# Sliding-window attention: one turned block of summed probabilities, and values as block and difference

## The chip, the core and the metric

The kernel runs on one core of a Trainium2 chip. The metric is the device time of one launch in microseconds (us); lower is better. Engines are called as the profile calls them: PE (TensorE), DVE (VectorE), ACT (ScalarE), POOL (GpSimd), SP (the queue that issues most DMAs). A time written as "at 245 us" counts from the start of the profiled span.

## What is computed

One inference step of one layer of a hybrid decoder for a prompt of 1024 tokens and 8 sequences of 4 sample tokens. The input is normalised and modulated by a condition, multiplied by one wide matrix (`w_in`), and goes through two branches: an mLSTM (matrix memory, 4 heads, chunks of 128 tokens) and an attention over a sliding window (8 query heads in groups of 4 over 2 key heads, head size 64, window 128, with a learned sink per head). Both are gated, multiplied by their output matrices and merged, and a last matrix and norm give `y`. The change touches the prompt's attention alone:

```python
dist = q_pos[:, :, None] - k_pos[:, None, :]
mask = (dist >= 0) & (dist < WINDOW) & (k_pos[:, None, :] >= 0)
s = jnp.where(mask[None, :, None, None], s, -jnp.inf)
mx = jnp.maximum(jnp.max(s, axis=-1, keepdims=True), sink)
p = jnp.exp(s - mx)
den = jnp.sum(p, axis=-1, keepdims=True) + jnp.exp(sink - mx)
o = jnp.einsum('bnkgqs,bnskd->bnqkgd', p / den, v.astype(f32))
```

A block of 128 queries sees two blocks of keys, the preceding one ("far") and its own ("near"). With window 128, query i sees the far keys j > i and the near keys j <= i. So in each row the two masks are complementary: where one block has a probability, the other has zero.

## The kernel before

The program is one long instruction stream, written by Python code. The large products run one after another on PE: the keys and values (`ak`, `av`), four query jobs (`aq` 0 to 3), eight jobs for the memory heads (`mq`, `mk`, `mv`), and from about 282 us pairs of jobs done as seven block products each (`block_products`, `Pair`), then the output matrices. Each job is 8 x 3 products for each of three pieces of columns (`piece`).

Everything smaller is fed in between by a planner, the class `Side`. It holds generators in streams: "m" (the chain of gate factors, then the four memory heads), "a" (`kv_turn`, then 16 attention units), "x" (`sum_blocks` and later loads), "s" (sample attention, then four sample heads), "g" (`ada_gate`). A stream has a maximum of generators alive and a least gap between two starts. A generator yields a lag and the PSUM banks that its next visit needs; the planner keeps its own clock, `side.now`, which products advance by estimated durations (`mm`, `tr`), and at each `tick` steps those generators whose lag has passed and whose banks are free by its own reckoning. So the order of PE's instructions is fixed when the program is written. `side.until(condition)` advances the planner's clock without large products until the condition holds; `hook` calls it ahead of the block products that read `sum_blocks`' operands ("t2", "t1"), ahead of the query gates (all 16 units done), and ahead of the head gates (enough sample heads done: five for the last).

PSUM has four pairs of banks, tagged `g`, `a`, `b` and `o`. Tiles of SBUF with tag `half` come from 43 buffers. `store` puts a DMA off by 4.0 of the planner's clock; `dma` issues at once, after any put-off store to the same tensor.

A `unit(g, b0)` does two query blocks of query group g, for both key heads (kv 0 and 1):

1. loads of the queries (`q`, in `qv`), three key blocks (`kT`) and the value blocks (`vn`, one in `kv_`, two in `qv`); lag 12.0
2. four score products into banks `a`; DVE adds the mask and takes maxima; then `nmx`
3. ACT: exponentials with sums (`den`)
4. DVE: `den` and its reciprocal; probabilities times 1/den, kv 0 on DVE, kv 1 on ACT, 256 columns each; lag 7.0
5. eight transposes (six where b0 = 0, which has no far block for its first query block), four for each kv into a bank `b`; ACT and DVE copy them back
6. eight products with values (six where b0 = 0) into a bank `o`; ACT copies, and the result is stored.

`kv_turn` transposes the values once for all units and keeps them in DRAM (`vnD`).

A memory `head(h)` goes through its chunks in three groups (loads, `prep`, `stage_a` to `stage_c3`), each a chain of small operations on ACT and DVE with products in between; the sample heads start when the last of the four is done.

Of the kernel before, what the change touches and what calls it, by code (L numbers as in the profile page):

```python
# [10 lines left out]
F32 = mybir.dt.float32  # L11
# [100 lines left out]
class Side:  # L112
# [4 lines left out]
    def __init__(self, each, limits, quiet):  # L117
        self.each, self.free = each, {}
        self.now, self.last, self.quiet, self.products = 0.0, 0.0, quiet, 0
        self.streams = {n: {"max": m, "gap": g, "wait": [], "live": [], "next": 0.0} for n, (m, g) in limits.items()}  # L120

    def add(self, stream, gen, banks=""):
# [15 lines left out]

    def tick(self):
        self.each()  # L140
        for st in self.streams.values():
            if st["wait"] and len(st["live"]) < st["max"] and self.now >= st["next"]:
                self.begin(st)
        used, visit = set(), self.now >= self.last + self.quiet
        for item in sorted((i for st in self.streams.values() for i in st["live"]), key=lambda i: i[1]):
            banks = set(item[2])
            if self.now < item[1] or used & banks or (banks and not visit) or any(self.now < self.free.get(b, 0) for b in banks):
                continue
            used |= banks
            for b in banks:  # L150
                self.free[b] = self.now + (6.0 if "+" in banks else HOLD[b])
            n = self.products
            self.step(item)
            if self.products > n:
                self.last = self.now
# [17 lines left out]
def body(tc, a):  # L173
    nc = tc.nc
    with ExitStack() as ctx:
# [11 lines left out]
        def pb(shape, name):  # L187
            return ps.tile(shape, F32, tag="b", bufs=2, name=name)
# [52 lines left out]
        def dma(out, in_, late=False):  # L241
            stores(in_.tensor)
            issue(out, in_, late)

        def issue(out, in_, late=False):
            ins = nc.sync.dma_start(out, in_)
            ins = getattr(ins, "ins", ins)
# [5 lines left out]
        side = Side(stores, {"m": (2, 35.0), "a": (5,8.0), "x": (2, 0.0), "s": (1, 0.0), "g": (1, 0.0)}, 1.5)  # L253
        def mm(out, lhsT, rhs, start, stop, share=1, more=False):
            n = int(np.prod(rhs.shape[1:]))
            side.now += max(n, 250) / 2400 if rhs.dtype == F32R else max(n * 4 // share, 128) / 2400
            side.products += 1
            in_order(nc.tensor.matmul(out, lhsT, rhs, start=start, stop=stop, skip_group_check=more))  # L258

        def tr(out, in_, idn):  # L260
            side.now += 0.11
            side.products += 1
            in_order(nc.tensor.transpose(out, in_, idn))
# [460 lines left out]
        def by_block(t):  # L724
            return t.rearrange("p (c q e) -> p c q e", q=4, e=32)
# [14 lines left out]
        kD, vnD = dp.tile([128, SEQ], F32, name="kD"), dp.tile([128, 8, 128], F32, name="vnD")  # L740
        qD = [dp.tile([128, SEQ], F32, name=f"qD{g}") for g in range(4)]

        def rope_load(p):
# [30 lines left out]
        def kv_turn():  # L774
            kl, kTs, vT, kns, vns = at.pop("kl"), at["kTs"], at.pop("vT"), ht([128, 128], "kns")[:NS], at["vns"]
            for p, n in enumerate((3, 3, 2)):
                tp = pb([128, 3, 128], f"vtp{p}")
                for j in range(n):
                    tr(tp[:, j], vT[p][:, j * 128:(j + 1) * 128], ident)
                vn = ht([128, 3, 128], f"avn{p}")  # L780
                S.copy(vn[:, :n], tp[:, :n])
                dma(vnD[:, 3 * p:3 * p + n], vn[:, :n])
                if p < 2:
                    yield 4.0, "b"
            dma(a["v_p"], vn[:, 1])
# [12 lines left out]
            dma(a["v_s"][124:128].rearrange("t b e -> b t e"), vns)  # L798
# [8 lines left out]
        def unit(g, b0):  # L807
# [2 lines left out]
            n0 = 1 if b0 == 0 else 0  # L810
            qv, kv_ = ht([128, 4, 128], "uqv"), ht([128, 4, 128], "ukv")
            q, kT = qv[:, 0:2].rearrange("p c e -> p (c e)"), kv_[:, 0:3].rearrange("p c e -> p (c e)")
            vn = kv_[:, 3], qv[:, 2], qv[:, 3]
            dma(q, qD[g][:, b0 * 128:b0 * 128 + 256])
            dma(kT[:, n0 * 128:], kD[:, (b0 - 1 + n0) * 128:(b0 + 2) * 128])
            dma(qv[:, 2:4], vnD[:, b0:b0 + 2])
            if b0:
                dma(vn[0], vnD[:, b0 - 1])
            yield 12.0, sc_bank[1]
            p = [ht([128, 2, 256], f"p{kv}") for kv in range(2)]  # L820
            mx = sm([128, 4], "mx", 3)
# [16 lines left out]
            for kv in range(2):  # L838
                for i, lo in enumerate(los):
                    j = 2 * kv + i  # L840
                    S.activation(p[kv][:, i, lo:], p[kv][:, i, lo:], AF.Exp, bias=nmx[:, j:j + 1],
                                 accum_out=den[:, j:j + 1])
            yield 3.0, ""
            V.tensor_tensor(den, den, nmx[:, 4:8], op=ALU.add)
            V.reciprocal(den, den)
            for kv in range(2):
                for i, lo in enumerate(los):
                    j = 2 * kv + i
                    if kv:
                        S.activation(p[kv][:, i, lo:], p[kv][:, i, lo:], AF.Copy, scale=den[:, j:j + 1])  # L850
                    else:
                        V.tensor_scalar(p[kv][:, i, lo:], p[kv][:, i, lo:], den[:, j:j + 1], None, op0=ALU.mult)
            yield 7.0, "b"
            pT = [t.rearrange("p i (j e) -> p (i j) e", e=128) for t in p]
            for kv in range(2):
                pt = pb([128, 4, 128], f"pt{g}_{b0}_{kv}")
                for j in range(n0, 4):
                    tr(pt[:, j], p[kv][:, j // 2, j % 2 * 128:j % 2 * 128 + 128], ident)
                if kv:
                    V.tensor_copy(pT[kv][:, n0:], pt[:, n0:])  # L860
                else:
                    S.copy(pT[kv][:, n0:], pt[:, n0:])
            yield 5.0, "o"
            oT = po([128, 2, 128], f"oT{g}_{b0}")
            for j in range(n0, 4):
                i, hf = divmod(j, 2)
                for kv in range(2):
                    r = slice(64 * kv, 64 * kv + 64)
                    mm(oT[r, i], vn[i + hf][:, r], pT[kv][:, j], start=(hf == 0 or b0 + i == 0), stop=(hf == 1))
            c0 = b0 * 128  # L870
            o = qv[:, 0:2].rearrange("p c e -> p (c e)")
            S.copy(o, oT.rearrange("p c e -> p (c e)"))
            store(oD[g][:, c0:c0 + 256], o)
            units_done.append((g, b0))
# [146 lines left out]
        def across(h, n, src, c0):  # L1021
            m = src.shape[1]
            t = ht([128, 512], f"{n}t")[:, :m]
            V.transpose(t, src)
            for b in range(0, 128, 32):
                nc.gpsimd.dma_start(mN[n][h][c0:c0 + m, b:b + 32].rearrange("(t p) e -> p t e", p=32), t[b:b + 32].rearrange("p (t e) -> p t e", e=32))  # L1026

        def head(h):
            an, wend, dec, fl = st["an"], st["wend"], st["dec"], st["fl"]
# [88 lines left out]
            def stage_c3(p):  # L1118
                m = len(GROUPS[p])
                ns, (d, r) = w_[p]  # L1120
                for i in range(m):
                    V.tensor_scalar(ns[:, i, 0:128], ns[:, i, 0:128], d[:, i:i + 1], r[:, i:i + 1], op0=ALU.mult, op1=ALU.mult)
                y = ht([128, 384], "yt")[:, :m * 128]
                V.transpose(y.rearrange("p (c e) -> p c e", e=128), ns[:, :m, 0:128])
                c0 = GROUPS[p][0]
                for b in range(4):
                    nc.gpsimd.dma_start(yhD[h][c0:c0 + m].rearrange("c (q i) (b e) -> b i c q e", i=32, e=32)[b], by_block(y[32 * b:32 * b + 32]))  # L1127
# [607 lines left out]
        def hook(n, i):  # L1735
# [404 lines left out]
```

## Time and profile before

| | |
|---|---|
| time, median of 3 runs | 861.15 us (860.39 to 861.27) |
| time of the profiled execution | 857.75 us |
| its span, first to last instruction | 855.9 us |
| mean granted PE clock | 0.992 |
| instructions | 15332 |
| transposes in the units (`pt`) | 120, from 111.2 to 260.4 us |
| value products in the units (`oT`) | 240 instructions, from 118.0 to 274.1 us |

The profile's page gives for each engine its busy time and its share of the span; then the span in 40 slices, a digit being the busy share of a slice in tenths (9 for 90% or more). A line of a group reads: source line, engine, operation, output<-inputs, shapes, count | busy us, mean ns | idle time of the engine ahead of it, and what ended it. A line of one tile gives durations as min/median/max ns, and the first and last start. A line of the timeline gives start, duration, engine and operation, and in brackets the idle time before it with its releaser. Waits are listed as engine and tile <- what released it: total us, number, longest. Nearly all operations are recorded in a helper, so they share the line of it (L219, L246, L258, L263) and are told apart by their tiles.

### The profile page before, as it was taken

The numbers are of one execution on the slowest core, as the hardware profiler recorded it, in microseconds if no ns is written. First come the engines' busy times: TensorE is split into PE (matmuls) and PEld (weight loads), VectorE is DVE, ScalarE is ACT, GpSimd is POOL, SyncE is SP. The second block draws the span as 40 slices with busy tenths as digits, with TensorE's granted clock in tenths as the row PEclk, the third lists the DMA queues.
The fourth block names the chain that finished last, engine by engine and source line by source line (L and its number), as shares of the span: only waits on it lengthen the run. The fifth ranks groups of instructions, "written<-read, shape, count | busy, mean of one in ns | idle before, by whom it ended". The sixth has DMA issues, their size and how long they took to land. (4 is left out here: it accounts for less than half of the span.)

```text
span 855.9 us, 15332 instructions
## 1 busy us (share of the span) xinstructions
PE 822.3 (96%) x5139; PEld 686.6 (80%) x5139; DVE 604.1 (71%) x1596; ACT 390.5 (46%) x963; POOL 174.7 (20%) x236
## 2 busy tenths in 40 slices
PE   6899999999999989999999999999999999999984
PEld 3689988789789778888887777777788999967863
DVE  3787785555687778668666565978766669857987
ACT  4672356545564543555444454434443333233334
POOL 0220000330341434211111000000012032532563
PEclk9999999999999999999999999999999999999998
DMA  9995549459756765664444335553436974273322
GB/s 326 366 356 183 150 137 291 134 125 294 214 153 203 214 170 151 194 198 135 129 115 130 115 111 162 160 150 89 116 99 203 345 254 137 82 247 99 111 99 104
DMA packets 125347, 150.82 MB, mean 176 GB/s; under 512 B 29057, under 2 KB 81409, under 8 KB 125237
## 3 DMA queue, kind: packets, MB, share of 16 engines
q1 hardware_dynamic: 121044, 143.55, 53.5%
q0 software_dynamic: 4224, 6.30, 3.6%
q8 instruction: 40, 0.66, 0.3%
q14 instruction: 39, 0.31, 0.1%
HBM read 109.73 MB, written 41.08 MB: 176 GB/s over the span
## 5 line engine op out<-in xcount | busy, mean ns | idle before, releaser
L1127 POOL DMA_DIRECT2D yhD<-yt x48 | 28.9, 608 | 108.3 <-DVE yt L219 86.3
L258 PE MATMUL g_w_ao<-ya,wh_w_ao 128*128 128x384 f32 (+1 forms) x192 | 45.7, 322 | 0.1
L258 PE MATMUL g_w_mo<-ym_l,wh_w_mo 128*128 128x384 f32 (+1 forms) x192 | 45.7, 323 | 0.0
L219 ACT ACTIVATE p<-p,nmx 128x256 f32<-128x256 f32 (+1 forms) x64 | 31.0, 486 | 28.3 <-DVE nmx L219 28.3
L1026 POOL DMA_DIRECT2D mkN<-mkt x44 | 26.9, 618 | 45.5 <-DVE mkt L219 26.0
L219 DVE CUSTOM_DVE_ANT_0 p<-sc,cst,sink 128x256 f32<-128x256 f32 (+1 forms) x64 | 26.1, 463 | 11.4 <-PE sc L258 11.4
L258 PEld LDWEIGHTS g_w_ao<-ya,wh_w_ao 128*128 128x128 f32 x192 | 33.5, 188 | 0.7 <-DVE ya L219 0.6
L258 PEld LDWEIGHTS g_w_mo<-ym_l,wh_w_mo 128*128 128x128 f32 x192 | 33.5, 188 | 0.0
L258 PE MATMUL g_aq<-h_h,wh_aq 128*128 128x384 f32 (+1 forms) x96 | 32.5, 338 | 0.0
L1026 POOL DMA_DIRECT2D mvN<-mvt x40 | 24.7, 624 | 33.6 <-DVE mvt L219 12.5
L258 PE MATMUL g_aq<-h_l,wh_aq 128*128 128x384 f32 (+1 forms) x96 | 31.0, 323 | 0.0
L258 PE MATMUL g_w_mo<-ym_l,wl_w_mo 128*128 128x384 f32 (+1 forms) x96 | 31.0, 323 | 0.0
L258 PE MATMUL g_aq<-h_h,wl_aq 128*128 128x384 f32 (+1 forms) x96 | 31.0, 323 | 0.0
L258 PE MATMUL g_w_ao<-ya,wl_w_ao 128*128 128x384 f32 (+1 forms) x96 | 30.8, 321 | 0.0
L258 PE MATMUL g_mq<-h_h,wh_mq 128*128 128x384 f32 (+1 forms) x72 | 24.7, 344 | 0.8 <-ACT vs L219 0.8
L258 PE MATMUL g_mk<-h_h,wh_mk 128*128 128x384 f32 (+1 forms) x72 | 24.8, 344 | 0.0
L219 POOL TENSOR_TENSOR ya<-yr,ya 128x384 fp32r<-128x384 f32 (+1 forms) x6 | 7.3, 1222 | 80.7 <-DVE hg L219 67.4
L258 PE MATMUL g_mk<-h_l,wh_mk 128*128 128x384 f32 (+1 forms) x72 | 23.2, 323 | 0.0
L258 PE MATMUL g_mk<-h_h,wl_mk 128*128 128x384 f32 (+1 forms) x72 | 23.2, 323 | 0.0
L258 PE MATMUL g_mq<-h_h,wl_mq 128*128 128x384 f32 (+1 forms) x72 | 23.2, 322 | 0.0
L258 PE MATMUL g_mq<-h_l,wh_mq 128*128 128x384 f32 (+1 forms) x72 | 23.2, 322 | 0.0
L219 POOL COPY qs<-mk 128x32 f32<-128x32 f32 x3 | 1.4, 463 | 103.1 <-ACT mk L219 103.1
(1700 smaller groups left out, 2800.9 us busy)
## 6 DMA issues: line engine op xcount, KB each, us to landing
hb<-hD SPq DMA_DIRECT2D x24, 256.0 KB
x<-xT SPq DMA_DIRECT2D x16, 256.0 KB
early_h<-w_ada SPq DMA_DIRECT2D x8, 512.0 KB
hD<-x SPq DMA_DIRECT2D x16, 256.0 KB
adar_ga<-w_ada SPq DMA_DIRECT2D x16, 256.0 KB
wr_ga<-w SPq DMA_DIRECT2D x16, 256.0 KB
wr_gm<-w SPq DMA_DIRECT2D x16, 256.0 KB
taD<-gt SPq DMA_DIRECT2D x16, 256.0 KB
```

Source lines behind the costliest of these rows:

```text
L219: ins = f(*args, **kw)
L258: in_order(nc.tensor.matmul(out, lhsT, rhs, start=start, stop=stop, skip_group_check=more))
L1026: nc.gpsimd.dma_start(mN[n][h][c0:c0 + m, b:b + 32].rearrange("(t p) e -> p t e", p=32), t[b:b + 32].rearrange("p (t e) -> p t e", e=32))
L1127: nc.gpsimd.dma_start(yhD[h][c0:c0 + m].rearrange("c (q i) (b e) -> b i c q e", i=32, e=32)[b], by_block(y[32 * b:32 * b + 32]))
```

## The change

In `unit`, for each key head and query block, the far block is scaled by 1/den on ACT, and one DVE operation scales the near block and adds the far one. The sum is a single block of 128x128, since the two never overlap. It is transposed once: four transposes in one bank `b` for a whole unit. The transposed block is read twice: ACT copies it (`both`), and DVE multiplies it by the triangle `tri` (one where the key's index is at most the query's), which keeps the near part (`near`). The output is `both` times the values of the preceding block, plus `near` times the difference (own block minus preceding block). A query block with no far block uses `near` alone, and the difference of the first block is the block itself.

`kv_turn` makes the differences and stores blocks and differences side by side in DRAM (`vdD`, nine places of two). A unit loads its four (or three) blocks in one DMA, issued after the exponentials, into the tile that held the queries. The output goes through the tile of the keys.

The order changes too: units start every 7.0 instead of 8.0 of the planner's clock, and the lag ahead of the transposes is 5.0 instead of 7.0; `ada_gate` is added after the second query job instead of after the fourth; and a stream can be held: "m" starts no further generator while one is alive and fewer than 16 units are done. `put` and `scatter` keep a tally of queue times; `landed` is not called, and the DMAs that they issue are the same.

```diff
+        self.held = {}
...
+            held = name in self.held and self.held[name]()
-            if st["wait"] and len(st["live"]) < st["max"] and self.now >= st["next"]:
+            if st["wait"] and not held and len(st["live"]) < st["max"] and self.now >= st["next"]:
...
-        side = Side(stores, {"m": (2, 35.0), "a": (5,8.0), ...
+        side = Side(stores, {"m": (2, 35.0), "a": (5, 7.0), ...
...
-                dma(vnD[:, 3 * p:3 * p + n], vn[:, :n])
+                dv = ht([128, 3, 128], f"adv{p}")
+                if p:
+                    V.tensor_tensor(dv[:, 0], vn[:, 0], before[:, 2], op=ALU.subtract)
+                else:
+                    V.tensor_copy(dv[:, 0], vn[:, 0])
+                V.tensor_tensor(dv[:, 1:n], vn[:, 1:n], vn[:, 0:n - 1], op=ALU.subtract)
+                store(vdD[:, 3 * p + 1:3 * p + 1 + n, 0], vn[:, :n])
+                store(vdD[:, 3 * p:3 * p + n, 1], dv[:, :n])
+                before = vn
...
-            vn = kv_[:, 3], qv[:, 2], qv[:, 3]
-            dma(qv[:, 2:4], vnD[:, b0:b0 + 2])
-            if b0:
-                dma(vn[0], vnD[:, b0 - 1])
...
+            dma(qv[:, n0:], vdD[:, b0:b0 + 2].rearrange("p b t e -> p (b t) e")[:, n0:])
             yield 3.0, ""
             V.tensor_tensor(den, den, nmx[:, 4:8], op=ALU.add)
             V.reciprocal(den, den)
             for kv in range(2):
                 for i, lo in enumerate(los):
-                    j = 2 * kv + i
-                    if kv:
-                        S.activation(p[kv][:, i, lo:], p[kv][:, i, lo:], AF.Copy, scale=den[:, j:j + 1])
+                    d, near, far = den[:, 2 * kv + i:2 * kv + i + 1], p[kv][:, i, 128:], p[kv][:, i, 0:128]
+                    to = p[0][:, i, 0:128] if kv else near
+                    if lo:
+                        V.tensor_scalar(to, near, d, None, op0=ALU.mult)
                     else:
-                        V.tensor_scalar(p[kv][:, i, lo:], p[kv][:, i, lo:], den[:, j:j + 1], None, op0=ALU.mult)
-            yield 7.0, "b"
-            pT = [t.rearrange("p i (j e) -> p (i j) e", e=128) for t in p]
-            for kv in range(2):
-                pt = pb([128, 4, 128], f"pt{g}_{b0}_{kv}")
-                for j in range(n0, 4):
-                    tr(pt[:, j], p[kv][:, j // 2, j % 2 * 128:j % 2 * 128 + 128], ident)
-                if kv:
-                    V.tensor_copy(pT[kv][:, n0:], pt[:, n0:])
-                else:
-                    S.copy(pT[kv][:, n0:], pt[:, n0:])
+                        S.activation(far, far, AF.Copy, scale=d)
+                        V.scalar_tensor_tensor(to, near, d, far, op0=ALU.mult, op1=ALU.add)
+            yield 5.0, "b"
+            pt = pb([128, 2, 2, 128], f"pt{g}_{b0}")
+            for i in range(2):
+                for kv in range(2):
+                    tr(pt[:, i, 1 - kv], p[0][:, i, 128 * (1 - kv):128 * (2 - kv)], ident)
+            both, near = (t.rearrange("p i (k e) -> p i k e", e=128) for t in p[::-1])
+            S.copy(both, pt)
+            V.tensor_tensor(near, pt, tri.unsqueeze(1).unsqueeze(1).to_broadcast((128, 2, 2, 128)), op=ALU.mult)
             yield 5.0, "o"
...
-                    mm(oT[r, i], vn[i + hf][:, r], pT[kv][:, j], start=(hf == 0 or b0 + i == 0), stop=(hf == 1))
+                        mm(oT[r, i], qv[:, v, r], w[:, i, 1 - kv], start=(w is both or bool(lo)), stop=(w is near))
...
-            o = qv[:, 0:2].rearrange("p c e -> p (c e)")
+            o = kv_[:, 0:2].rearrange("p c e -> p (c e)")
...
+        side.held["m"] = lambda: len(side.streams["m"]["live"]) > 0 and len(units_done) < 16
...
         for g in range(4):
             queries(g)
-        side.add("g", ada_gate())
+            if g == 1:
+                side.add("g", ada_gate())
```

More of the change, by code (lines that the diff above doesn't have):

```diff
@@ L140, in tick @@
         self.each()
-        for st in self.streams.values():
-            if st["wait"] and len(st["live"]) < st["max"] and self.now >= st["next"]:
+        for name, st in self.streams.items():
+            held = name in self.held and self.held[name]()
+            if st["wait"] and not held and len(st["live"]) < st["max"] and self.now >= st["next"]:
                 self.begin(st)
@@ L243, in dma, with put, landed, scatter @@
             issue(out, in_, late)
+        queue = {"sync": 0.0, "gpsimd": 0.0}
+        def put(eng, cost):
+            queue[eng] = max(queue[eng], side.now) + cost
+        def landed(eng, least):
+            return max(least, queue[eng] - side.now + (2.5 if eng == "sync" else 4.0))
+        def scatter(out, in_):
+            nc.gpsimd.dma_start(out, in_)
+            put("gpsimd", 0.65)
         def issue(out, in_, late=False):
             ins = nc.sync.dma_start(out, in_)
+            put("sync", 0.42)
             ins = getattr(ins, "ins", ins)
@@ L251, in issue @@
             free.append(ins)
-        side = Side(stores, {"m": (2, 35.0), "a": (5,8.0), "x": (2, 0.0), "s": (1, 0.0), "g": (1, 0.0)}, 1.5)
+        side = Side(stores, {"m": (2, 35.0), "a": (5, 7.0), "x": (2, 0.0), "s": (1, 0.0), "g": (1, 0.0)}, 1.5)
         def mm(out, lhsT, rhs, start, stop, share=1, more=False):
@@ L738, in attention_begin @@
             at["vns"] = cp.tile([NS, 128], F32, name="vns")
-        kD, vnD = dp.tile([128, SEQ], F32, name="kD"), dp.tile([128, 8, 128], F32, name="vnD")
+        kD, vdD = dp.tile([128, SEQ], F32, name="kD"), dp.tile([128, 9, 2, 128], F32, name="vdD")
         qD = [dp.tile([128, SEQ], F32, name=f"qD{g}") for g in range(4)]
@@ L863, in unit @@
+            both, near = (t.rearrange("p i (k e) -> p i k e", e=128) for t in p[::-1])
+            S.copy(both, pt)
+            V.tensor_tensor(near, pt, tri.unsqueeze(1).unsqueeze(1).to_broadcast((128, 2, 2, 128)), op=ALU.mult)
             yield 5.0, "o"
             oT = po([128, 2, 128], f"oT{g}_{b0}")
[L865 to L868, printed above, removed]
-                    mm(oT[r, i], vn[i + hf][:, r], pT[kv][:, j], start=(hf == 0 or b0 + i == 0), stop=(hf == 1))
+            for i, lo in enumerate(los):
+                for v, w in ((2 * i, both), (2 * i + 1, near))[bool(lo):]:
+                    for kv in range(2):
+                        r = slice(64 * kv, 64 * kv + 64)
+                        mm(oT[r, i], qv[:, v, r], w[:, i, 1 - kv], start=(w is both or bool(lo)), stop=(w is near))
@@ L1025, in across @@
             for b in range(0, 128, 32):
-                nc.gpsimd.dma_start(mN[n][h][c0:c0 + m, b:b + 32].rearrange("(t p) e -> p t e", p=32), t[b:b + 32].rearrange("p (t e) -> p t e", e=32))
+                scatter(mN[n][h][c0:c0 + m, b:b + 32].rearrange("(t p) e -> p t e", p=32), t[b:b + 32].rearrange("p (t e) -> p t e", e=32))
         def head(h):
@@ L1126, in stage_c3 @@
                 for b in range(4):
-                    nc.gpsimd.dma_start(yhD[h][c0:c0 + m].rearrange("c (q i) (b e) -> b i c q e", i=32, e=32)[b], by_block(y[32 * b:32 * b + 32]))
+                    scatter(yhD[h][c0:c0 + m].rearrange("c (q i) (b e) -> b i c q e", i=32, e=32)[b], by_block(y[32 * b:32 * b + 32]))
             for visit in ([(load, 0), 10.0, ""], [(prep, 0), 3.0, "o"], [(stage_e, 0), (stage_a, 0), 5.0, "o"],
```

## The prediction

> **What bounds the kernel now.** I read the page's busy shares and its 40 slices first, then a table by stage, then who waits for whom on TensorE.
>
> ```profile
> span 855.9 us, 15332 instructions
> PE 822.3 (96%) x5139; PEld 686.6 (80%) x5139; DVE 604.1 (71%) x1596; ACT 390.5 (46%) x963; POOL 174.7 (20%) x236
> PE   6899999999999989999999999999999999999984
> ```
>
> TensorE (PE) is busy in 96% of the span, and its row of slices dips only at the start, in slice 15 (300 to 321 us), and at the end. The table by stage follows (window, its length, then busy time and instructions of PE, weight loads, VectorE, ScalarE, GpSimd, then the granted clock, DMA share, GB/s).
>
> ```profile
> 60.00:86.00 26.00, 26.00 (x197) 23.16 (x196) 19.64 (x63) 8.16 (x20) 0.19 (x1) 1.00 0.65 209
> 86.00:122.10 36.10, 36.10 (x238) 32.84 (x237) 29.40 (x112) 15.34 (x50) 0.00 (x0) 1.00 0.48 136
> 204.30:282.30 78.00, 76.48 (x593) 67.94 (x591) 56.08 (x181) 42.48 (x129) 24.88 (x42) 1.00 0.71 200
> 282.30:306.00 23.70, 20.23 (x125) 16.56 (x124) 18.78 (x68) 11.84 (x34) 8.15 (x15) 0.93 0.82 237
> 306.00:654.00 348.00, 347.22 (x2031) 277.44 (x2030) 242.74 (x624) 161.78 (x373) 40.72 (x76) 1.00 0.49 142
> ```
>
> The attention units lie between 86 and 275 us. There PE is full or within 1.5 us of it, so an instruction taken from PE shortens the program by its slot, as long as the other engines still deliver in time. From 306 to 654 us PE is full as well, so what is won earlier is carried through. The one loose place is 282 to 306 us. PE's waits say what ends there:
>
> ```profile
> PE foX L258 <- ACT foW L219: 3.9, 2, 3.7
> PE bx L258 <- DVE f3r_w L219: 2.3, 1, 2.3
> PE pt L263 <- ACT p L219: 1.5, 2, 0.8
> ...
> PE bw L258 <- DVE t2l L219: 1.2, 1, 1.2
> ```
>
> Two waits for VectorE (2.3 and 1.2 us) belong to the join of the fused stage with the block products. The 3.9 us are the tail, which the change does not touch. The 1.5 us are inside the transposes that the change halves.
>
> **The change, part by part.** First the transposes.
>
> ```profile
> L263 PE MATMUL pt<-cst,p x120: 270/272/331, 111.2 to 260.4; 128*128 128x128 f32 x120
> 127.21 1.03 PE L263 MATMUL pt<-cst,p 128*128 128x128 f32 x8
> 159.30 0.60 PE L263 MATMUL pt<-cst,p 128*128 128x128 f32 x4
> ```
>
> There are 120: 8 in each of 12 units, 6 in each of the 4 units with b0 = 0. Afterwards every unit has 4, together 64, so 56 go. A row of 272 ns is not the price, since transposes overlap. Eight of them took 1.03 us of which the last is 0.272, so seven steps took 0.76 us: 0.108 us each. 56 x 0.108 = 6.0 us, all of it on the bound engine.
>
> The Trainium skill, page "TensorE: Matmul & The Clock Gate", Part 4 "PE-mode transpose", gives about 275 ns for a transpose inside a kernel. The row's 272 ns agrees with it as a duration; used as a price it would make 56 x 0.275 = 15.4 us (an estimate from that page). The start-to-start step decides, so the sum keeps 6.0.
>
> Second, the bank. Before, a unit takes two of the two `b` banks in one visit; afterwards one. In the unit at 159.30 four transposes were issued, then PE stood until ScalarE freed the second bank:
>
> ```profile
> 160.72 0.66 PE L263 MATMUL pt<-cst,p 128*128 128x128 f32 x4 [0.82 <-ACT p L219]
> ```
>
> The fifth could have started at 159.30 + 4 x 0.108 = 159.73 and started at 160.72, so 0.99 us were lost where the idle column says 0.82. Scaled to the 1.5 us of both such waits: 1.8 us. With one bank a unit waits for one release only, so I take 1.8 as gone; bounds 0 and 1.8.
>
> Third, the products with the values. The count is the same (8 in a full unit, 6 with b0 = 0; the trace shows each fp32 one as two instructions), with the same 64 weight columns and 128 moving columns, so PE pays nothing:
>
> ```profile
> L258 PE MATMUL oT<-p,uqv x192: 272/273/324, 118.0 to 274.1; 128*64 128x128 f32 x192
> L219 ACT ACTIVATE p<-p,den 128x256 f32<-128x256 f32 x28 | 13.0, 500 | 3.9 <-DVE den L219 2.5 <-DVE mr L219 1.4
> L219 ACT ACTIVATE p<-p,den 128x128 f32<-128x128 f32 x4 | 1.6, 403 | 2.8 <-DVE den L219 2.7
> L219 DVE TENSOR_SCALAR p<-p,den 128x256 f32<-128x256 f32 x28 | 9.4, 354 | 0.3
> L219 DVE TENSOR_SCALAR p<-p,den 128x128 f32<-128x128 f32 x4 | 1.1, 287 | 0.1
> L219 DVE SCALAR_TENSOR_TENSOR C<-C,dec,U 128x129 f32<-128x129 f32 x28 | 9.7, 345 | 0.6 <-PE n L258 0.2
> L219 DVE COPY p<-pt 128x512 f32<-128x512 f32 x12 | 8.2, 686 | 3.7 <-PE pt L263 3.6
> L219 DVE TENSOR_TENSOR gt<-p,by 128x512 f32<-128x512 f32 x8 | 5.5, 686 | 7.6 <-PE by L258 7.6
> ```
>
> Fourth, the normalising. ScalarE had 2 x 0.500 us in a full unit and gets 4 x 0.403: +0.61. VectorE had 2 x 0.354 and gets four scale-and-add operations of 128 columns. The trace has none on SBUF alone; the nearest rows are 0.287 (one operand) and 0.345 (129 columns, one operand in PSUM). I take 0.345: 4 x 0.345 - 0.71 = +0.67; with 0.287, +0.44. Units with b0 = 0 gain about the same on VectorE (+0.62) and nothing on ScalarE. VectorE's copy out of PSUM becomes a multiplication by the triangle out of PSUM, 0.686 for 0.686. Over 16 units that is +10 to 11 us of VectorE and +7 of ScalarE, beside PE. What covers it is the time between normalising and transposing. The shortest such time was
>
> ```profile
> 123.05 0.34 DVE L219 TENSOR_SCALAR p<-p,den 128x256 f32<-128x256 f32 x1
> 130.70 1.04 PE L263 MATMUL pt<-cst,p 128*128 128x128 f32 x8
> ```
>
> 7.3 us. The chain grows by 0.6 + 0.35 us, and the visit comes 2.0 sooner on the planner's clock (`yield 7.0` to `5.0`). That clock runs slow against the chip's:
>
> ```profile
> L258 PE MATMUL sc<-ukv,uqv x128: 272/376/481, 94.9 to 243.2; 64*128 64x256 f32 x112, 64*128 64x128 f32 x16
> 86.05 0.38 SPq L246 DMA_DIRECT2D uqv<-qD  x1
> ```
>
> From the first unit's scores at 94.9 to the last one's at 242.4 (0.8 us ahead of its last instruction) 15 gaps of 8.0 took 147.5 us, 1.23 us for each of the planner's, so 2.0 are 2.5 us. 7.3 - 0.95 - 2.5 leaves 3.9 us: cost zero.
>
> Fifth, the loads. Two value loads a unit (one where b0 = 0) become one, issued after the exponentials into the place of the queries.
>
> ```profile
> L246 SPq DMA_DIRECT2D uqv<-vnD x16: 319/423/1195, 87.0 to 231.5; - x16
> L246 SPq DMA_DIRECT2D ukv<-vnD x12: 320/422/1314, 89.7 to 232.0; - x12
> ```
>
> SP issues 12 fewer of 0.42 us and three more stores in `kv_turn`. The load now waits until the scores have read the queries, and SP works in order, so weight loads, the next unit's q and k loads and the gate's loads queue behind it. A unit's own loads went out at 86.05 for scores at 94.9, 8.8 us ahead, and the value load has 13 x 1.23 = 16 us until its product. GpSimd's queue keeps its issues. A wait of a few us on SP is covered; cost zero, upper bound one lost lead, about 2 us of PE. `kv_turn` adds six small VectorE operations, 0.29 to 0.43 us each, about 2 us, in 60 to 86 us, where VectorE has 6.4 us free: zero.
>
> Sixth, the order. `a` starts units every 7.0 instead of 8.0, so the last begins up to 18 us sooner. `ada_gate` starts two query jobs earlier. `held` keeps a second head back until 16 units are done. Before, head 1 loaded at 244.52, and units ended at 274.1; afterwards they end between 253 and 274, and head 1 slides there. Does the end of the heads move?
>
> ```profile
> 244.52 0.34 SPq L246 DMA_DIRECT2D hq<-qD  x1
> 314.65 0.43 SPq L246 DMA_DIRECT2D hq<-qD  x1
> L263 PE MATMUL sty<-cst,sns x4: 242/243/244, 493.3 to 622.0; 32*128 32x32 f32 x4
> 640.13 0.39 PE L258 MATMUL bw<-t2h,wh_phead_gate__7542 128*128 128x512 f32 x1
> ```
>
> Head 2 loads at 314.65, once its values exist; 35 x 1.23 = 43 us after head 1's new start is 296 to 317, so heads 2 and 3 stay. And the last sample head ended at 622.0 where the last gate asks for it at 640.13: 18 us of cover. Cost zero.
>
> At the join the new order works both ways. PE arrives sooner while `sum_blocks` keeps its own pace; but one head's VectorE work has left that place. I take zero there and price both signs below.
>
> The sum: 6.0 + 1.8 = 7.8 us. The profiled execution took 857.75 (855.9 of span and 1.85 around it), so 849.9. The median of the runs is 861.15, 3.4 above it; on that footing 853.3. A difference under 0.2% (1.7 us) cannot be told from none.
>
> **The rivals.** What one lost wait costs is seen in the clock:
>
> ```profile
> 302.40:305.80 3.40, 3.40 (x13) 2.93 (x12) 3.40 (x10) 1.24 (x2) 2.19 (x4) 0.50 0.84 245
> ```
>
> Right behind the 2.3 us wait PE had half its clock for 3.4 us, so it lost 1.7 more: such a wait costs 4.0.
>
> The Trainium skill, "TensorE: Matmul & The Clock Gate", Part 1, "What's actually happening", puts the drop behind an idle window of about 3.4 us. By that rule a wait of 2.3 would cost 2.3; here a 2.3 us wait was followed by the drop, so the trace decides.
>
> (a) The join gets looser: 2.3 + 1.7 + 1.2 = 5.2 us more go, 848. For it: the 2.3 us wait stands behind `f3r_w`, a head's chain, and `held` moves a head. Against: head 0's chain stays.
>
> ```profile
> L219 DVE TENSOR_TENSOR hb<-hb,hb x16: 649/691/693, 211.4 to 303.7; 128x512 f32<-128x512 f32 x16
> L219 DVE CUSTOM_DVE_ANT_0 p<-sc,cst,sink 128x256 f32<-128x256 f32 x56 | 24.2, 480 | 8.4 <-PE sc L258 8.4
> 121.32 0.17 DVE L219 RECIPROCAL den<-den 128x4 f32<-128x4 f32 x1
> ```
>
> (b) The gain is partly or wholly given back at the join. `sum_blocks` forms its operands with VectorE operations of 0.69 us, six for each of four blocks (16.6 us), at its own pace; if it isn't sooner, PE waits there for what it won: 861, or 863 with the clock; half of it is 857.
>
> (c) The other side: VectorE becomes the bound in the dense stretch at 86 to 122 us. It is busy 29.40 of 36.10. A unit costs it 4 x 0.48 for the masked maxima, 0.71 and 0.69 as above, and four small ones of 0.17: 4.0, afterwards 4.7; three units become 3.4: 16.0 for 12.0, so 33.4 of 36.1. It decides once another 2.7 us of work falls into that stretch. Then weight splits come late, each wait with its clock drop is 4.0, two cancel the gain and three make 853.3 + 12 = 865. Against it: PE shows no wait at all there today.
>
> **How the numbers follow.** Forecast (853.3, own range 851 to 855.5) 0.52; (a) 0.13; (b) in part, 855.5 to 859, 0.13, wholly 0.09; (c) 0.13. Faster is 0.52 + 0.13 + 0.13 = 0.78, same 0.09, slower 0.13. The range runs from (a) to just short of (b) wholly: 847.5 to 860.5.
>
> **What would show it.** 64 transposes, no `pt` wait on `p`; `oT` still 240; units ending about 255 to 265; the two VectorE waits at the join, and whether the half clock follows; head 3's sample part still ahead of the last gate. The prediction is wrong if PE shows new waits at 86 to 205 us for `wl` or `p` tiles, or if the wait at the join grows.

## The result, and the profile after

| | before | after |
|---|---|---|
| median of 4 runs each | 860.77 us (858.84 to 861.27) | 850.25 us (849.69 to 851.53) |
| ratio of the means, 95% interval | | 0.9884 (0.9864 to 0.9904) |
| profiled execution (span) | 857.75 us (855.9) | 851.53 us (849.7) |

The change made the kernel about 10 us faster; 7.8 was forecast. A second comparison, in a later series, gave 0.9903 (0.9876 to 0.993), 8.0 us of median (858.77 to 850.75). The two traces differ by 6.2 us only: the profiled execution of before lies 3.0 us under its median, and that of after is the slowest of its four, 1.3 over its median. So the account below, made from traces, covers 6 us of the 8 to 10; where the rest lies is not shown.

The page of after, its span, busy shares and the slices of TensorE:

```profile
span 849.7 us, 15293 instructions
PE 816.6 (96%) x5083; PEld 681.2 (80%) x5083; DVE 614.9 (72%) x1634; ACT 393.9 (46%) x987; POOL 172.9 (20%) x236
PE   6899999999999899999999999999999999999984
```

PE lost 56 instructions (5139 to 5083) and 5.7 us of busy time. VectorE gained 10.8 us (10 to 11 was forecast) and ScalarE 3.4 (7 was forecast from single durations; 56 of 395 ns are 22.1 us, but they overlap and keep the engine busy for 18.6), and the span still fell. The dip moved from slice 15 to slice 14 (276 to 297 us).

By the tiles of the units and by form, after:

```profile
L278 PE MATMUL pt<-cst,p x64: 270/272/329, 109.1 to 248.0; 128*128 128x128 f32 x64
L273 PE MATMUL oT<-p,uqv x240: 272/273/324, 115.7 to 255.8; 128*64 128x128 f32 x120
L221 DVE TENSOR_TENSOR p<-pt,cst x16: 652/684/693, 111.9 to 249.3; 128x512 f32<-128x512 f32 x16
L221 DVE SCALAR_TENSOR_TENSOR p<-p,den 128x128 f32<-128x128 f32 x56 | 17.5, 346 | 2.9 <-ACT p L221 2.2 <-issue 0.2
L221 ACT ACTIVATE p<-p,den 128x128 f32<-128x128 f32 x56 | 18.6, 395 | 6.5 <-DVE den L221 6.5
```

There are 64 transposes and still 240 value products; the scale-and-add takes 0.346 us; the units end at 255.8 us. PE's waits from the units on, after:

```profile
PE foX L273 <- ACT foW L221: 4.2, 2, 4.0
PE n L273 <- DVE C L221: 2.8, 1, 2.8
PE U L273 <- DVE et L221: 1.7, 1, 1.7
...
PE bw L273 <- ACT bw L221: 1.1, 2, 0.7
```

No wait is inside the transposes any more, and the waits for `f3r_w` and `t2l` at the join are gone. Two others stand in their place, for `C` and `et` of the memory heads.

To see where the time goes I cut one stretch out of every trace: from the first product of the query jobs to the first product of the tail's sums (`foX`). Its length is PE's idle time, plus what half clock costs (half of PE's busy time in the rows where the granted clock is 0.50), plus the rest, which is work at full clock. By windows, the stretch and the join of before (its half clock is the prediction's row at 302.40, 3.40 us with PE busy throughout), then those of after, with its half clock and the dense stretch of the units:

```profile
65.23:747.23 682.00, 675.32 (x4351) 577.65 (x4343) 478.04 (x1328) 310.24 (x796) 115.12 (x178) 1.00 0.57 167
272.00:306.00 34.00, 30.53 (x220) 26.24 (x209) 27.63 (x92) 15.39 (x41) 14.71 (x25) 0.95 0.73 200
```

```profile
65.23:740.83 675.60, 669.12 (x4296) 572.24 (x4287) 488.76 (x1366) 313.64 (x820) 113.83 (x178) 0.99 0.58 171
279.10:285.93 6.83, 4.66 (x15) 4.08 (x16) 6.04 (x18) 2.88 (x11) 4.42 (x9) 0.50 0.81 114
272.00:306.00 34.00, 29.45 (x167) 24.36 (x166) 30.31 (x101) 15.44 (x39) 12.21 (x21) 0.90 0.63 168
86.00:122.10 36.10, 36.10 (x238) 32.58 (x238) 30.57 (x118) 16.22 (x55) 0.00 (x0) 1.00 0.73 202
```

Before: 682.00 - 675.32 = 6.68 idle, 3.4 / 2 = 1.70 for the half clock, and 673.62 of work. After: 6.48, 4.66 / 2 = 2.33, and 666.79. So the work fell by 6.8 us, the idle time by 0.2, and the half clock took 0.6 more: 6.4 us in this stretch. Over 272 to 306 us, the join, PE's idle time grew from 3.47 to 4.55 us.

### The profile page after: what moved, and what is told of

It is laid out like the page before. It is cut to its first block, busy times and chain, and to the rows that moved or that the text cites. A ratio compares the mean times of both kernels' runs of the same rounds, so it can differ in the third digit from the quotient of the medians.

```text
span 849.7 us, 15293 instructions
## 1 busy us (share of the span) xinstructions
PE 816.6 (96%) x5083; PEld 681.2 (80%) x5083; DVE 614.9 (72%) x1634; ACT 393.9 (46%) x987; POOL 172.9 (20%) x236
## 5 line engine op out<-in xcount | busy, mean ns | idle before, releaser
L273 PEld LDWEIGHTS g_w_ao<-ya,wh_w_ao 128*128 128x128 f32 x192 | 33.4, 188 | 0.7 <-DVE ya L221 0.6
```

## The experiments

The same account for every kernel (us; "half clock" is what it costs). The experiments ran in three series of four, each on a chip of its own; every ratio is to runs of before in the same series, and the stretch is that of one profiled execution:

| kernel | ratio to before (95%) | median | stretch | idle | half clock | work |
|---|---|---|---|---|---|---|
| before, again | 1.0002 (0.9989 to 1.0015) | 859.19 | 681.61 | 7.87 | 0 | 673.74 |
| after, again | 0.9903 (0.9876 to 0.993) | 850.75 | 675.13 | 6.90 | 1.70 | 666.53 |
| block, old order | 1.0001 (0.999 to 1.0012) | 859.20 | 681.79 | 11.27 | 2.88 | 667.64 |
| new order, old blocks | 1.0026 (1.0013 to 1.004) | 861.23 | 685.80 | 8.90 | 3.41 | 673.49 |
| after, each turned twice | 0.9986 (0.997 to 1.0003) | 857.91 | 684.27 | 7.88 | 3.03 | 673.36 |
| after, no hold | 0.9884 (0.9867 to 0.9902) | 848.38 | 673.55 | 5.61 | 0 | 667.94 |
| after, gap 8 | 0.9981 (0.9969 to 0.9994) | 856.78 | 677.88 | 8.99 | 0 | 668.89 |
| after, gate late | 0.9926 (0.9906 to 0.9946) | 851.82 | 674.52 | 5.10 | 1.70 | 667.72 |
| after, sums early | 0.9917 (0.9898 to 0.9936) | 851.44 | 674.30 | 6.05 | 0 | 668.25 |
| block, old order, gap 7 | 1.0004 (0.9995 to 1.0012) | 859.18 | 681.65 | 8.96 | 3.41 | 669.28 |
| before, half turned | 0.993 (0.9904 to 0.9955) | 852.42 | 678.72 | 8.74 | 3.41 | 666.57 |
| after, no hold, sums early | 0.9847 (0.9834 to 0.986) | 845.53 | 669.94 | 3.18 | 0 | 666.76 |

### The block alone, in the old order

Diff from after:

```diff
-  "a": (5, 7.0)
+  "a": (5, 8.0)
-            yield 5.0, "b"
+            yield 7.0, "b"
-        side.held["m"] = lambda: ...
-            if g == 1:
-                side.add("g", ada_gate())
+        side.add("g", ada_gate())
```

> The summed block, the single turn and the value differences, with the order put back: units every 8.0, lag 7.0 ahead of the transposes, the gate job after the fourth query job, no held stream. Theory 1 (the gain is PE's slots: 56 transposes at 0.108 us and the 1.8 us of second-bank waits): 7.8 us less than before, ratio 0.991, with 64 transposes and no wait of pt on p. Theory 2 (a good part of the gain comes from the new order, which moves VectorE work of a head away from the join at 282 to 306 us): 4 to 6 us less, ratio 0.993 to 0.995, and the order alone gives the rest. Theory 3 (without the new order the join gets worse, since PE comes earlier and the sums of blocks do not): 2 to 5 us less.

It came out equal to before: 1.0001, where all three theories had a gain. The work of the stretch is as short as in after (667.64), but 4.6 us more of idle time and 1.2 more of half clock take it back. Windows of this kernel:

```profile
65.49:747.28 681.79, 670.52 (x4297) 572.85 (x4288) 488.32 (x1366) 314.35 (x820) 113.93 (x178) 0.99 0.58 169
240.00:256.00 16.00, 11.59 (x57) 11.14 (x56) 13.23 (x44) 7.40 (x22) 2.48 (x5) 0.79 0.71 212
248.90:255.73 6.83, 5.76 (x19) 5.67 (x20) 5.51 (x13) 2.77 (x9) 2.32 (x4) 0.50 0.89 276
```

From 240 to 256 us PE stands for 4.4 of 16 us. Its timeline there, PE, VectorE and ScalarE in order of time:

```profile
239.93 0.29 PE L273 MATMUL g_mv<-h_h,wl_mv 128*128 128x288 f32 x1
...
247.10 0.16 DVE L221 TENSOR_TENSOR den<-den,nmx 128x4 f32<-128x4 f32 x1 [1.17 <-ACT p L221]
...
248.21 0.34 DVE L221 SCALAR_TENSOR_TENSOR p<-p,den 128x128 f32<-128x128 f32 x1
248.64 0.69 DVE L221 TENSOR_TENSOR t3l<-hb,t3h 128x512 fp32r<-128x512 f32 x1
249.25 0.44 DVE L221 STREAM_TRANSPOSE mvt<-g_mv 128x256 f32<-128x256 f32 x1
249.73 0.18 ACT L221 COPY vs<-g_mv 128x32 f32<-128x32 f32 x1 [0.23 <-DVE mvt L221]
249.97 0.69 PE L273 MATMUL g_mq<-h_h,wh_mq 128*128 128x384 f32 x1 [4.41 <-ACT vs L221]
```

The `mv` job filled its bank at 240.2 us. The bank comes free once VectorE has transposed it (`mvt`) and ScalarE has copied the last piece (`vs`). But `mvt` starts 9 us later. VectorE takes its operations in the written order: it stood idle for 1.17 us ahead of 247.10, waiting for ScalarE's exponentials, while `mvt` had its input since 240.2. Ahead of `mvt` lie operations of a unit, of a head (`et`, `C`) and one of `sum_blocks` (`t3l`). PE goes on with the next piece in the other bank and then stops for 4.4 us, and 6.8 us at half clock begin inside that wait. PE had arrived here 7.8 us earlier than before (240.07 for 247.91, the next piece's first product); at the start of the block products it was 0.4 us ahead. Before had this wait too, at 255.2 us, but short:

```profile
PE g_mq L258 <- ACT vs L219: 0.8, 1, 0.8
```

There `mvt` came 6.4 us after its bank was full, behind a head's operations that waited for their loads. With the half clock behind it this bank costs PE 0.8 us in before and 4.4 + 2.9 = 7.3 in this kernel. In after the same transposition starts as soon as its products end:

```profile
241.57 0.44 DVE L221 STREAM_TRANSPOSE mvt<-g_mv 128x256 f32<-128x256 f32 x1
```

### The new order alone

The four order edits of the change (gap, lag, hold, gate) in before, blocks untouched.

> The kernel before with the new order alone: units every 7.0, lag 5.0, the gate job after the second query job, the stream of heads held. Eight transposes a unit and two banks as before. Theory 1: within 1.7 us of before (0.998 to 1.002). Theory 2: 3 to 5 us less (0.994 to 0.997), from the waits at the join. Theory 3: slower by 1 to 4 us, because units packed closer wait more often for their second bank.

1.0026: a little slower. The order is worth nothing by itself, and makes the difference between no gain and the whole gain once the block is there. The third theory had the size but not the place: PE's waits for a second bank at the transposes were 0.6 us here, for 1.5 in before. The longest waits from the units to the tail are these:

```profile
PE bx L260 <- DVE mvt L221: 2.5, 1, 2.5
PE bx L260 <- DVE zt L221: 2.5, 1, 2.5
```

Both are in the block products, and each was followed by 3.41 us at half clock.

### Every transpose issued twice

```diff
             tr(pt[:, i, 1 - kv], ...)
+            in_order(nc.tensor.transpose(pt[:, i, 1 - kv], ...))
```

The second issue writes the same values and is not counted on the planner's clock, so the written order stays.

> The changed kernel with every transpose of a unit issued a second time to the same place (64 more), in the same planned order, since the planner's clock does not count the second one. Theory 1: 64 x 0.108 = 6.9 us more than the changed kernel, so 0.9965 of before, about 857. If transposes cost their 0.272 us each it is 17 us more (1.008 of before). If PE's slack takes them up (the join decides), under 3 us more (0.992).

0.9986, 7.7 us of median above after. Against the nine traces with the block and single transposes (work 666.53 to 669.28, mean 667.76) the 64 extra transposes lengthen the work to 673.36: 5.6 us or 0.088 each; against after alone 6.6 us or 0.103. The forecast price was 0.108; the nine traces themselves spread by 2.8 us. The other part of the loss is idle time and half clock, 2.1 us more than in after.

### Before once more

No edit: what two runs of one text may differ by.

> The kernel before, unchanged: a second profile of it, and what two series of the same kernel differ by. Its first profiled execution took 857.75 us while the runs had a median of 860.8, and the changed kernel's profiled one 851.53 with a median of 850.25, so the two traces differ by 6.2 us and the medians by 10.5. If the clock's drops behind waits are what varies, this profile shows more time at half clock than the first (3.4 us at 302 us and 3.4 us at 825 us), and about 860 us; if the first was typical, 857 to 858 with the same drops.

1.0002, within its interval of nothing. In its trace the wait ahead of the join was followed by no half clock.

### After without the hold

```diff
-        side.held["m"] = lambda: len(side.streams["m"]["live"]) > 0 and len(units_done) < 16
```

> The changed kernel without the held stream: a second head may start while units are still open. Theory A (holding the second head keeps its VectorE chain away from 245 to 300 us, and that is what lets the saved slots through): most of the gain is lost, 0.995 to 1.000 of before, with waits of PE for VectorE of 3 us and more between 245 and 300 us. Theory B (what counts is that the units are over before the bank release at 250 us and the join, so the shorter gap does it): 0.986 to 0.990, as the changed kernel.

0.9884, as fast as after. The hold is not what makes the order fit.

### After with the old gap

```diff
-  "a": (5, 7.0)
+  "a": (5, 8.0)
```

> The changed kernel with units started every 8.0 again. Theory B: the wait that the summed block alone showed at 250 us (4.4 us and 3.4 us of half clock), where the release of a bank by mv stands behind a unit's normalising on VectorE, is back: 0.996 to 1.001 of before. Theory A: 0.988 to 0.992.

0.9981: most of the gain is gone. Work is 668.89, idle 8.99. The time is in theory B's range, but the wait that B expected at 250 us is not there: from 240 to 256 us PE is busy throughout. Its longest waits lie behind 285 us:

```profile
PE by L273 <- ACT by L221: 2.7, 1, 2.7
PE bx L273 <- ACT hg L221: 1.7, 1, 1.7
```

So the bank at 250 us is not the one place that takes a gain back.

### After with the gate at its old place

```diff
-            if g == 1:
-                side.add("g", ada_gate())
+        side.add("g", ada_gate())
```

> The changed kernel with the gate job added after the fourth query job again. Both theories: its 32 products and two bank visits only move, so within 0.3% of the changed kernel, 0.986 to 0.992 of before. If it shares the b banks with the units at the wrong time, a wait of 1 to 4 us at 200 to 260 us and 0.990 to 0.995.

0.9926: the interval lies above that of the first comparison and overlaps that of the second (up to 0.993). A part of the gain may hang on it, not much.

### After with the sums begun one job earlier

`sum_blocks` is added five jobs before the block products instead of four:

```diff
-                if i == -4:
+                if i == -5:
```

> The changed kernel with sum_blocks added one job earlier (at mq of head 1, not mk of head 1), so that its operands are ready ahead of the join. In the trace of the changed kernel PE was 10.1 us ahead of before at 272 us and 5.1 at 287: 1.7 and 2.8 us of waits while the planner lets only heads step until the sums are formed, and 6.8 us at half clock. If this wait at the join takes back the gain: 4 to 8 us less than the changed kernel, 0.979 to 0.984 of before, and no half clock behind 275 us. If the heads' own chains are the limit there: within 1.7 us of the changed kernel (0.986 to 0.990). If the 24 tiles of the sums, held longer, take buffers from units and heads: slower, 0.991 and more.

0.9917: no gain over after, though the join was the suspected place and 4 to 8 us were expected from it. In its trace PE starts the block products 7.4 us ahead of before (after: 10.1) and ends the products with `t2` 9.7 ahead (after: 5.1), so the join did get looser. But at the end of the stretch it is 7.5 ahead; a wait of 2.5 us for `zt` stands at 553 us. The median did not move.

### The short gap alone with the block

Diff from the first experiment: only `"a": (5, 8.0)` to `(5, 7.0)`.

> The summed block with nothing of the new order but the gap: units every 7.0; lag 7.0, gate job after the fourth query job, no held stream. Theory B (the shorter gap alone lets the saved slots through): 0.988 to 0.993 of before, PE's waits between 204 and 740 us about 5 to 7 us in sum. If the gate job's place is needed too (with it late and the rest in place the kernel was 0.9926): 0.992 to 0.995. If only all four edits together do it: 0.996 to 1.001.

1.0004, in the range of "only all four edits together"; but the runs without the hold and with the late gate show that not all four are needed. The short gap alone doesn't bring it. PE's waits in this kernel:

```profile
PE n L273 <- DVE C L221: 3.0, 1, 3.0
PE g_mq L273 <- ACT mk L221: 2.8, 1, 2.8
```

Other waits, and a stretch as long (681.65 for 681.79). So the gap is needed and not sufficient.

### Before with half of its transposes

In before, the transposes of kv 1 are left out (60 of 120); its copy reads the block of kv 0, and the planner's clock is advanced as if they were there.

> The kernel before with the transposes of key head 1 left out (60 of 120; its copy reads the block of key head 0, so the second head's output is not the reference's); everything else, the planner's order and clock included, as before. If freed slots count for themselves: 60 x 0.108 + 1.8 = 8.3 us less, 0.990 of before, and then it is the longer normalising and the shifted order of the summed block that give its gain back. If PE arriving earlier at the bank release at 250 us and at the join is what gives it back: 0.996 to 1.001, with PE's waits grown by 4 to 8 us from 240 to 310 us.

0.993: of 7 us less work (666.57 for 673.62, 0.118 for each of 60) about 6 reach the time. Its waits:

```profile
PE g_mq L258 <- ACT vs L219: 3.4, 1, 3.4
PE bx L258 <- DVE f3r_w L219: 2.4, 1, 2.4
PE bw L258 <- DVE t2l L219: 1.6, 1, 1.6
```

The first is the wait of the first experiment, a microsecond shorter: with its half clock 3.4 + 1.7 = 5.1 us, for 7.3 there. So in the old order slots alone already meet that bank, and the runs still gain 6 us; what the block loses in the old order is not lost by PE's early arrival alone. The block differs from this kernel in its longer normalising, its later value loads, and an order of its own, since the planner's clock counts fewer transposes. Which of these costs the 7 us of median between the two kernels was not separated; their traces differ by 3.1 us of stretch only.

### After again

> The changed kernel, unchanged: a second profile, and a ratio beside the others of this series. Its first profile had 6.5 us of waits and 6.8 us of half clock between the first query product and the last stage, and was the slowest of its four executions. Expected: 0.987 to 0.990 of before, and in the profile the same waits near 277 and 281 us with 0 to 6.8 us of half clock behind them. If the profile is 848 us or less with no half clock, the clock's drop is a matter of the execution and not of the kernel.

0.9903, its runs from 846.64 to 855.59. One text spreads over 9 us here; before, on the same chip, over 3.7 (857.0 to 860.72).

### No hold, and the sums earlier

```diff
-                if i == -4:
+                if i == -5:
...
-        side.held["m"] = lambda: len(side.streams["m"]["live"]) > 0 and len(units_done) < 16
```

> The changed kernel without the held stream and with the sums of blocks one job earlier. Without the hold the waits in the middle of the trace came to 5.6 us, with early sums to 6.1 us, of which 2.5 lie in one place at 553 us. If the two add up: waits of 3 to 4 us and 0.984 to 0.986 of before. If the heads' chains only move on to another place: 0.988 to 0.992, with a wait of 2 us or more behind 300 us.

0.9847 (844.67 to 846.81): the fastest of all, about 13 us under before and below both kernels' intervals. Its stretch, the join, and PE's waits from the units to the tail:

```profile
64.72:734.66 669.94, 666.76 (x4296) 570.30 (x4287) 489.08 (x1366) 314.22 (x820) 114.45 (x178) 1.00 0.58 172
272.00:306.00 34.00, 32.79 (x195) 27.02 (x194) 30.99 (x99) 16.21 (x42) 14.20 (x25) 1.00 0.59 166
```

```profile
PE g_mv L273 <- ACT mk L221: 1.1, 2, 0.7
...
PE bw L273 <- ACT bw L221: 0.7, 1, 0.7
```

In the stretch no wait is above 0.7 us, and there is no half clock. Its work is that of after (666.76 for 666.79): all that it wins over after's trace, 5.7 us, is idle time and half clock. Of the two edits alone neither showed a gain over after. The 5.7 us are read from one trace of each; the medians (850.75 for after again) differ by 5.2.

## Why the prediction was right, and which step was not

The direction and the range (847.5 to 860.5) held. The median came 3 us under the forecast of 853.3 and 0.75 under the likeliest case's own range (851 to 855.5), and the 7.8 us lie near the 8.0 and 10.5 of the two comparisons. That the sum came so close is in part luck: of its two terms only the first is found again in the traces, and it holds only because the change brought an order that the sum had at zero.

**Transposes (6.0 us).** Right. The work of the stretch fell from 673.6 (before twice, new order alone) to 667.76, the mean of nine traces with the block: 5.9 us, within a spread of 2.8 us among those nine traces. Twice-issued and left-out transposes price one at 0.09 to 0.12 us; 0.108 was taken from the start-to-start step. The row of 0.272 us would have made 15 us of it, which no run shows.

**The second bank (1.8 us).** The waits went, as said; the time did not: PE's idle time in the stretch fell by 0.2 us only (with the second trace of each, from a mean of 7.3 to 6.7, while the half clock grew from 0.9 to 2.0). The waits at the join took it.

**Value products, normalising, loads (zero).** Right in the new order; in the old one the block as a whole gained nothing, so there zero is not shown. 240 products as before; 0.346 us for 0.345 taken. In 86 to 122 us VectorE is busy 30.57 of 36.10 and PE all of it, so the rival with VectorE as the bound fell. The cover ahead of the transposes was thinner than worked out: the shortest time from the last normalising to the transposes is 2.1 us (114.4 to 116.5) where 3.9 was taken, and no transpose waits. As for the rival, its forecast of 33.4 counted 4.0 us of added work, where VectorE's operations on the units' `p` tiles rose by 2.4 there. The same stretch with tile `p` alone, before and then after (the columns are PE, weight loads, VectorE, ScalarE):

```profile
86.00:122.10 36.10, 1.69 (x18) 1.35 (x18) 6.52 (x17) 9.09 (x31) 1.00 0.48 136
```

```profile
86.00:122.10 36.10, 2.06 (x20) 1.55 (x20) 8.95 (x23) 10.51 (x35) 1.00 0.73 202
```

The value loads after:

```profile
L260 SPq DMA_DIRECT2D uqv<-vdD x16: 319/326/524, 98.8 to 233.5; - x16
```

No product waits for them. At the other end, the last sample head and the last gate's products for it, after:

```profile
L278 PE MATMUL sty<-cst,sns x4: 243/244/244, 494.9 to 619.6; 32*128 32x32 f32 x4
633.74 0.39 PE L273 MATMUL bw<-t2h,wh_phead_gate__7526 128*128 128x512 f32 x1
```

14 us of cover where 18 were. The heads did not move the end.

**The order (zero).** This step failed, though the sum did not show it. It priced the order as a term of its own, and "cost zero" is true of that: alone it costs 0.26%. But the block's 7.8 us could only be booked because the order was there. With the block in the old order they come to nothing: in its trace PE, 7.8 us early, runs into a bank whose release stands on VectorE behind a unit and a head, and loses 7.3 us there. The wait was in the profile of before with 0.8 us, and the prediction did not ask what an earlier PE makes of it. Rival (b), the gain given back, did happen with the block alone, only not where I put it (the sums at the join) but 40 us ahead of it. That this bank is the whole cause is not shown: half turned meets it too and keeps 6 us, and with the old gap the gain goes without that wait.

**The join (zero).** This step failed too. The prediction named a growing wait at the join as a sign that it is wrong, and it grew: 3.47 to 4.55 us of idle time, and 2.33 for 1.70 of half clock. PE reached the block products 10.1 us ahead of before and ended those with `t2` 5.1 ahead. Its timeline after:

```profile
275.17 0.61 PE L273 MATMUL U<-hv,hkn 128*128 128x129 f32 x4
277.52 0.94 PE L273 MATMUL U<-hv,hkn 128*128 128x129 f32 x6 [1.74 <-DVE et L221]
...
281.27 0.80 PE L273 MATMUL n<-hv,et 128*128 128x129 f32 x2 [2.81 <-DVE C L221]
```

Both waits belong to the memory heads' chains. The second is head 0's last group: its `U` (two chunks, hence x4) was there at 275.8, and `C`, which VectorE makes from it, started at 280.49. What makes `C` late is again VectorE's order: ahead of it stand operations of both heads and, just before it, three of the block products' weights and sums. The first wait is head 1's first group (three chunks, x6), whose bank comes free with `et`. VectorE's timeline after:

```profile
278.71 0.65 DVE L221 TENSOR_TENSOR wl_phead_in__3738<-wr_mq,wh_phead_in__3737 128x512 fp32r<-128x512 f32 x1
279.29 0.68 DVE L221 TENSOR_TENSOR t3l<-hb,t3h 128x512 fp32r<-128x512 f32 x1
279.88 0.68 DVE L221 TENSOR_TENSOR ws<-wr_mv,wr_mv 128x512 f32<-128x512 f32 x1
280.49 0.73 DVE L221 SCALAR_TENSOR_TENSOR C<-C,dec,U 128x129 f32<-128x129 f32 x2
```

Without the hold head 1 comes sooner: its second group's queries load at 263.50 us for 273.65 in after, and the wait for `et` is gone. Head 0's `U` comes as before (275.05), and the wait for `C` is still 2.4 us in two parts; with the sums earlier too it is gone. So rival (a), the looser join, is there to be had, not in the changed kernel but in the last experiment.

What stays open: with the block, the old gap loses 7 to 8 us and the short gap alone gains nothing, so a second edit must be needed beside it, the lag of 5.0 or the early gate. The late gate costs little, which points to the lag; the lag was not tried alone, and neither was the hold with the late gate.

## What to carry to other kernels

On an engine that is busy 96% of the time, a removed instruction is worth its start-to-start step, and that price held. Whether the time falls by it is a second question: follow PE's next arrival at each bank and each join, a few microseconds earlier, and look what is written ahead of the releasing instruction on its engine; a short wait in the profile of before marks such a place. Edits of the work and edits of the order have to be measured together: here 0 and +2 us made -8 to -10, and two edits that showed no gain alone made -5.

## What was not expected of the hardware

Half clock comes in pieces of 3.41 or 6.83 us. Most stood behind waits of 2.3 to 3.4 us or began inside one (of 4.4 us in the block alone; of 2.8 us after one of 1.7 in after). With the late gate one stood behind four short ones (1.37, 0.45, 0.95 and 1.19 us). But waits of 2.19 (before again), 2.66 (the old gap), 2.52 (sums early) and 3.40 us (each turned twice) had none behind them. The Trainium skill, "TensorE: Matmul & The Clock Gate", "What's actually happening", gives a window of 3413 ns that runs freely; the lengths of one or two windows agree with it. Its condition, one idle window, does not hold here as an idle time of 3.4 us: 2.3 us of waiting were followed by the drop in one trace, and 3.40 were not in another. A wait's price thus varies: one piece adds 1.7 us and two in a row 2.3 to 3.0 (the table), and from one execution of a text to the next it can be absent (before and before again).

That does not explain how far the runs of one text spread. After again spreads from 846.64 to 855.59 in six runs and the last experiment from 844.67 to 846.81 in four, but the block in the old order, with 4.4 us of waiting and a half clock behind it, only from 858.41 to 860.22 in twelve. Nor does the granted clock: two runs of after again with a mean of 0.991 took 846.64 and 846.9 us, and two with 0.992 took 850.15 and 851.9. The cause stays open.
